# First weights in halves, ones ahead of them, and another order of the early pairs in four SwiGLUs

## The chip, the cores and the metric

The kernel runs on one core of one Trainium2 chip. The metric is the device time of one execution in microseconds. The engines are TensorE (PE in the profile, with PEld for its weight loads), VectorE (DVE), ScalarE (ACT), GpSimd (POOL) and SyncE (SP, which issues nearly all DMAs).

## The reference

A trunk of two layers over 768 tokens (512 of one group, 256 of another) with 1024 features. Each layer is a half SwiGLU, a mixer, and a half SwiGLU; a final RMSNorm ends it. The mixer of layer 0 is a gMLP gate beside windowed attention, that of layer 1 is a 2-D neighbourhood attention. Four SwiGLUs in all, with FF = 2816 hidden columns:

```python
def rmsnorm(x, g):
    x32 = x.astype(jnp.float32)
    y = x32 * lax.rsqrt(jnp.mean(x32 * x32, axis=-1, keepdims=True) + EPS)
    return y.astype(x.dtype) * g

def swiglu(h, wg, wu, wd):
    return (jax.nn.silu(h @ wg) * (h @ wu)) @ wd
...
# each half SwiGLU: x + 0.5 * swiglu(rmsnorm(x, g), wg, wu, wd)
```

## The kernel before

x is kept transposed as eight tiles x0 to x7 of 128 features by 768 tokens, worked on in two halves of H = 384 columns (HALVES). Every product is made of three fp32r matmuls: each operand is split into a high part and the rest, and high by high, low by high and high by low are summed in PSUM (mm3, L140). A weight tile of 128x512 is split by wsplit: ACT casts it to whi (L114), DVE subtracts to get wlo (L115).

In a SwiGLU (ffn) the hidden columns come as 11 pairs of two 128-column blocks, gate and up. A pair is a 2x2 block product (two feature halves, two token halves, two column blocks) done with seven products in place of eight. Its x operands are called b11, b21, t2, t3, n4, t1 and b22, each four tiles with a high part (b110h, ...) and a low part (b110l, ...); feed(m, 0) and feed(m, 1) make them for the two token halves. The weights of t2, t3, t1 and b22 are sums s1 to s4 of raw tiles (L609). One product is 24 matmuls of 128x384: two names, four feature tiles, three terms.

The operands carry the gains of the norm but not 1/rms, which is multiplied in later. norm_rt makes it: squares on ACT (L216, L219), added up on DVE (L220) into acc; a product with ones ("tok", norm_tok) sums over features; rsqrt is a chain of 128x3 operations on DVE (L265 to L276); norm_spread turns the result into diagonals (DVE L256 for the high part, ACT L254 for the rest) and spreads it over 128 partitions by a product onesr by diag in PE (the "spread"), which ACT copies to acc (L414). hidden(i, half) then multiplies the two finished PSUM banks by it on DVE: sg (L508) from the gate's, v (L510) from the up's, then silu on ACT and sg = sg * v (L511). These reads set the banks free.

Since 1/rms is late, the first EARLY = 4 pairs begin with b11 (p1, whose result ACT also copies to an SBUF tile, L524, and notes in copied) and b21 (p2), which accumulate in the banks "X", and only then hidden. Those are the stages that a generator yields between, and ORDER says whose stage comes next. There are four banks mm and four banks aux in PSUM; a pair takes two for X. Pair 3 takes aux for X, the others mm. After ORDER is through, the remaining products of pair 0, 1, ... follow, beginning with t2 and t3 in two further banks.

The order on PE is the order in which the code issues: self.t adds up a modelled time of the matmuls issued, and generators given to spawn (the norm's steps with their delays, second()) continue when their time has come. The order on DVE, ACT and SP is set by a scheduler with priorities (high_priority) and explicit followers (issue_after). second() makes the operands and squares of the second token half in the first SwiGLU. SP loads weights into four raw tiles (512 KB each); w tiles are five of each kind.

Of the kernel before, what the change touches and what calls it, by code (L numbers as in the profile page):

```python
# [9 lines left out]
F32 = mybir.dt.float32  # L10
# [3 lines left out]
AF = mybir.ActivationFunctionType  # L14
ALU = mybir.AluOpType

P = 128
D = 1024
KD = D // P
# [4 lines left out]
H = T // 2  # L24
# [6 lines left out]
KIND = {"l0f1": ("f", 0), "l0m": ("m0", 1), "l0f2": ("f", 2), "l1f1": ("f", 3), "l1m": ("m1", 4), "l1f2": ("f", 5)}  # L31
RPB_PAD = 24
NW = 5
DELAY0 = (7.0, 11.0)
DELAYM = (3.5, 7.5)
DELAY1 = (26.0, 12.0)
STEPS = (2.5, 1.5, 1.5)
RPB_W = 31 + 2 * RPB_PAD
NMASK = 8 * (24 + 32 + 24) + 4 * (40 + 40)
NE = 30  # L40
EARLY = 4
ORDER = (0, 1, 0, 1, 0, 2, 1, 3, 2, 3, 2, 3)

WTOTAL = 12 * D * FF + 8 * EARLY * P * D + D * 1792 + 2 * D * D + D * 3072 + D * 512
VTOK = (4.0,9.0)
# [6 lines left out]
class Trunk:  # L52
# [4 lines left out]
    def __init__(self, ctx, tc, aps, phases=PHASES):  # L57
        self.tc, self.nc, self.aps, self.phases = tc, tc.nc, aps, phases
        self.units = []
        self.woff = self.pi = 0  # L60
        self.t = 0.0
        self.chains = []
        self.spare = []
        self.first = []
        self.copied = []
        pool = lambda name, bufs, **kw: ctx.enter_context(tc.tile_pool(name=name, bufs=bufs, **kw))
# [22 lines left out]
        return side  # L89


    def raw(self, name, k0, nk, c0, n):
# [5 lines left out]
        raw = self.rawp.tile([P, nk * n], F32, tag="raw", name=f"raw{i}")  # L98
        self.nc.sync.dma_start(raw, src)
        if self.spare and i >= 16:  # L100
            self.spare.pop(0)()
        return raw.rearrange("p (k n) -> p k n", k=nk)

# [105 lines left out]
    def norm_add(self, m, c0, c1):  # L209

        nc = self.nc
        for a in range(c0, c1, H):
            b = min(a + H, c1)
            if a not in self.begun:
                self.begun.add(a)
                nc.scalar.activation(self.acc[:, a:b], self.x[m][:, a:b], AF.Square)  # L216
                continue
            sq = self.nt("sq")[:, : b - a]
            nc.scalar.activation(sq, self.x[m][:, a:b], AF.Square)  # L219
# [16 lines left out]

    def norm_spread(self, y, pool=None):

        nc = self.nc
        yh = self.sp.tile([P, 3], F32R, tag="yh", name="yh", bufs=2)  # L240
# [3 lines left out]
        rb = self.psum(self.aux, "aux")  # L244
        for i, t in enumerate((yh.bitcast(F32), yl)):
            diag = (
                pool.tile([P, H], F32R, tag="diag", name="diag", bufs=2)
                if pool and i
                else self.np_.tile([P, H], F32R, tag="nt", name="diag", bufs=3)
            )  # L250
            for b in range(3):
                c = slice(b * P, (b + 1) * P)
                if i:
                    nc.scalar.activation(diag[:, c], self.ident, AF.Copy, scale=t[:, b : b + 1])  # L254
                else:
                    nc.vector.tensor_scalar(  # L256
                        out=diag[:, c], in0=self.ident, scalar1=t[:, b : b + 1], scalar2=None, op0=ALU.mult
                    )
            self.mmul(rb[:, :H], self.onesr, diag, i == 0, i == 1)
        return rb[:, :H]  # L260

    def rsqrt(self, y, src, scale, v, h, it):

# [20 lines left out]
    def norm_half(self, h, d0=1.8, d1=4.0):  # L284

        c0, c1 = HALVES[h]
        yield d0
        with self.tc.high_priority():
            y = self.norm_tok(self.acc, c0, c1)
        yield d1  # L290
        with self.tc.high_priority():
            self.r[h] = self.norm_spread(y)

# [103 lines left out]
    def second(self):  # L397

        for n in (1, 2):
            while len(self.copied) < 2:  # L400
                yield 0.2
            with self.tc.issue_after(self.copied[1]):
                for m in [i // 2 + (0 if i % 2 else 4) for i in range(KD)]:
                    if n == 1:
                        self.feed(m, 1)
                    else:
                        self.norm_add(m, H, T)
        self.half_done(1)

    def norm_rt(self, h):  # L410

        yield from self.norm_half(h, *(DELAY1 if h else DELAY0))
        c0, c1 = HALVES[h]
        self.nc.scalar.copy(self.acc[:, c0:c1], self.r[h])  # L414
        self.scales.add(h)

    def ffn(self, pre):
        nc = self.nc
# [41 lines left out]
        def pair(p):  # L460

            early = p < EARLY
            names = ("gate", "up")
            a = {}

# [6 lines left out]
            h = hs[p] = {}  # L472
# [105 lines left out]
            last = (p1, p6, p2, p7, p4, p5, p3)  # L578
# [15 lines left out]
        kind = self.following[0]  # L594
# [814 lines left out]
    def build(self):  # L1409
        nc = self.nc  # L1410
        self.cp.tile([P, 96], F32, tag="space", name="space")
        self.ident = self.cp.tile([P, P], F32, tag="ident", name="ident")
        make_identity(nc, self.ident)
        self.ones = self.cp.tile([P, P], F32, tag="ones", name="ones")
        nc.gpsimd.memset(self.ones, 1.0)
# [3 lines left out]
        nc.scalar.dma_start(self.gains, self.aps["gains"])  # L1419
        self.ngains = self.cp.tile([P, 64], F32, tag="ngains", name="ngains")[:, : KD * len(NORMS)]  # L1420
        nc.gpsimd.tensor_scalar(out=self.ngains, in0=self.gains, scalar1=-1.0, scalar2=None, op0=ALU.mult)
        self.x = [self.xp.tile([P, T], F32, tag=f"x{m}", name=f"x{m}") for m in range(KD)]
        todo = [KIND[p] for p in self.phases] + [("last", 6)]
        kind = todo[0][0]
        if kind == "f":
            self.ffn_open("right")
            self.ffn_tiles()
# [1 line left out]
        elif kind != "last":  # L1429
            self.mixer_tiles("right")  # L1430
        self.norm_begin(todo[0])
        for h, (c0, c1) in enumerate(HALVES):
            for m in range(KD):
                nc.sync.dma_start(self.x[m][:, c0:c1], self.aps["x"][m, :, c0:c1])
                if not (h and kind == "f"):
                    self.final(m, c0, c1)
                if h == 0 and m % 4 == 3 and kind == "f":
                    pre = f"{self.phases[0][:2]}_ffn{self.phases[0][3]}"
# [126 lines left out]
```

## Time and profile before

| | |
|---|---|
| median of 3 runs | 2632.54 us (2632.37 to 2633.5) |
| profiled execution | 2634.87 us, span 2633.1 us, mean granted clock 0.99 |
| busy: PE, PEld, DVE, ACT, POOL | 97%, 95%, 86%, 52%, 3% |
| mean DMA rate | 84 GB/s over the span |
| first product of b11 in the first and in the fourth SwiGLU | 9.38 us, 2126.11 us |
| first spread in the second and in the third SwiGLU | 785.04 us, 1271.40 us |

A timeline row gives the start and the duration in us, the engine, the line, the operation with output <- inputs and shape, and in brackets the idle time before it with what ended it. A row of the waits gives the total, the count and the longest. A row of the windows gives, for a stretch, the busy us of PE, PEld, DVE, ACT and POOL with counts, then the granted clock of PE, the share of the DMA engines and GB/s.

### The profile page before, as it was taken

The numbers are of one execution on the slowest core, as the hardware profiler recorded it, in microseconds if no ns is written. First come the engines' busy times: TensorE is split into PE (matmuls) and PEld (weight loads), VectorE is DVE, ScalarE is ACT, GpSimd is POOL, SyncE is SP. The second block draws the span as 40 slices with busy tenths as digits, with TensorE's granted clock in tenths as the row PEclk, the third lists the DMA queues.
The fourth block names the chain that finished last, engine by engine and source line by source line (L and its number), as shares of the span: only waits on it lengthen the run. The fifth ranks groups of instructions, "written<-read, shape, count | busy, mean of one in ns | idle before, by whom it ended". The sixth has DMA issues, their size and how long they took to land.

```text
span 2633.1 us, 41175 instructions
## 1 busy us (share of the span) xinstructions
PE 2561.3 (97%) x15094; PEld 2491.3 (95%) x15094; DVE 2267.8 (86%) x4793; ACT 1365.6 (52%) x2851; POOL 88.0 (3%) x172
## 2 busy tenths in 40 slices
PE   7999999998999999999999999999999999999997
PEld 7999999987899999999999999989998989999997
DVE  8998889889779988898999888886777699988886
ACT  7544444555655544454654544454545465454443
POOL 0000000000100000000000000001222100000000
PEclk9999999999999999999999999999999999999998
DMA  5423222421223222222322222232221332222221
GB/s 168 133 78 103 71 81 65 145 87 37 89 77 97 81 81 77 68 75 86 96 81 81 73 73 74 88 111 63 63 63 40 105 104 81 81 71 74 68 87 54
DMA packets 83898, 218.99 MB, mean 83 GB/s; under 512 B 20080, under 2 KB 32880, under 8 KB 83696
## 3 DMA queue, kind: packets, MB, share of 16 engines
q1 hardware_dynamic: 83552, 216.34, 26.5%
q8 instruction: 118, 1.93, 0.3%
q14 instruction: 84, 0.69, 0.1%
q10 hardware_dynamic: 144, 0.03, 0.0%
HBM read 206.90 MB, written 15.07 MB: 84 GB/s over the span
## 4 chain that ended last, share of the span: by engine, by line
PE 86%; DVE 9%; ACT 2%; DMA 2%; issue 1%; SPq 0%; DVEq 0%; ACTq 0%
PE ps_mm L140 54%; PE ps_aux L140 31%; DMA raw<-in_w 1%; DVE wlo L115 1%; PE ps_aux L144 1%; DVE s L609 1%; DVE xl L739 1%; ACT p L911 1%; DVE p L920 0%; DVE p L905 0%; DVE tl L197 0%; ACT whi L114 0%; ACT xh L738 0%; DVE ol L197 0%; DVE x L706 0%
## 5 line engine op out<-in xcount | busy, mean ns | idle before, releaser
L114 ACT CAST whi<-s 128x512 fp32r<-128x512 f32 x496 | 304.9, 621 | 390.6 <-DVE s L609 133.1
L114 ACT CAST whi<-raw 128x512 fp32r<-128x512 f32 x512 | 311.0, 619 | 257.8 <-PE ps_mm L140 116.8
L115 DVE TENSOR_TENSOR wlo<-s,whi 128x512 fp32r<-128x512 f32 x496 | 337.0, 685 | 61.1 <-ACT whi L114 60.8
L115 DVE TENSOR_TENSOR wlo<-raw,whi 128x512 fp32r<-128x512 f32 x494 | 337.5, 691 | 28.3 <-ACT whi L114 24.1
L140 PE MATMUL ps_aux<-dt,whi 128*128 128x384 f32 x864 | 219.3, 334 | 2.1 <-ACT whi L114 2.1
L140 PE MATMUL ps_mm<-db,whi 128*128 128x384 f32 x864 | 219.2, 334 | 0.0
L140 PEld LDWEIGHTS ps_aux<-dt,whi 128*128 128x128 f32 x864 | 156.0, 188 | 2.4 <-ACT whi L114 2.4
L140 PEld LDWEIGHTS ps_mm<-db,whi 128*128 128x128 f32 x864 | 156.1, 188 | 0.0
L140 PE MATMUL ps_mm<-xh,whi 128*128 128x512 f32 (+1 forms) x416 | 147.4, 354 | 3.8 <-ACT xh L738 3.8
L140 PE MATMUL ps_aux<-dt,wlo 128*128 128x384 f32 x432 | 144.4, 334 | 0.3 <-DVE wlo L115 0.3
L140 PE MATMUL ps_mm<-db,wlo 128*128 128x384 f32 x432 | 144.4, 334 | 0.0
L140 PE MATMUL ps_mm<-xl,whi 128*128 128x512 f32 (+1 forms) x416 | 142.3, 342 | 1.1 <-DVE xl L739 1.1
L140 PE MATMUL ps_mm<-xh,wlo 128*128 128x512 f32 (+1 forms) x416 | 142.1, 341 | 0.0
L609 DVE TENSOR_TENSOR s<-raw 128x512 f32<-128x512 f32 x124 | 85.0, 686 | 23.0 <-DMA raw<-in_w 22.9
L499 DVE TENSOR_TENSOR u<-ps_aux,u 128x384 f32<-128x384 f32 x176 | 97.0, 551 | 2.8 <-PE ps_aux L140 2.6
L609 DVE TENSOR_TENSOR s<-raw,raw 128x512 f32<-128x512 f32 x124 | 83.7, 686 | 18.2 <-DMA raw<-in_w 18.0
L140 PE MATMUL ps_aux<-dh,whi 128*128 128x384 f32 x384 | 97.6, 335 | 0.6 <-DVE x L706 0.6
L911 ACT ACTIVATE p<-p,st 128x256 f32<-128x256 f32 (+3 forms) x144 | 68.9, 480 | 55.0 <-DVE st L909 54.9
L494 ACT COPY u<-ps_mm 128x384 f32<-128x384 f32 x176 | 83.5, 474 | 24.2 <-PE ps_mm L140 24.0
L661 DVE TENSOR_TENSOR x<-ps_aux,x 128x384 f32<-128x384 f32 x160 | 86.0, 552 | 9.3 <-PE ps_aux L140 9.2
L140 PEld LDWEIGHTS ps_mm<-xh,whi 128*128 128x128 f32 x416 | 79.9, 192 | 14.1 <-ACT xh L738 4.9
L140 PE MATMUL ps_mm<-oh,whi 128*128 128x384 f32 x256 | 88.1, 344 | 4.6 <-DVE x L888 4.0
(486 smaller groups left out, 8058.2 us busy)
## 6 DMA issues: line engine op xcount, KB each, us to landing
raw<-in_w SPq DMA_DIRECT2D x350, 512.0 KB, 3.7
xdm<-x SPq DMA_DIRECT2D x16, 384.0 KB, 2.3
x<-in_x SPq DMA_DIRECT2D x16, 192.0 KB, 5.5
x<-xdm SPq DMA_DIRECT2D x8, 384.0 KB, 3.4
xold<-xdm SPq DMA_DIRECT2D x8, 384.0 KB, 3.0
out_y<-y SPq DMA_DIRECT2D x8, 384.0 KB, 2.4
tab<-skew SPq DMA_DIRECT2D x8, 256.0 KB, 4.8
raw<-in_w SPq DMA_DIRECT2D x8, 256.0 KB, 2.6
```

What stands on the lines that cost most here:

```text
L114: nc.scalar.copy(hi, src)
L115: (eng or nc.gpsimd).tensor_tensor(out=lo, in0=src, in1=hi.bitcast(F32), op=ALU.subtract)
L140: self.nc.tensor.matmul(out, lhsT=lhsT, rhs=rhs, start=start, stop=stop, **kw)
L144: self.nc.tensor.transpose(out, src, self.ident)
L494: nc.scalar.copy(e[n, out], bank[key, n])
L499: nc.vector.tensor_tensor(out=t, in0=bank[key, n], in1=t, op=ALU.add)
L609: f = lambda o, x, y, op: self.nc.vector.tensor_tensor(out=o, in0=x, in1=y, op=op)
L661: nc.vector.tensor_tensor(out=o, in0=ps, in1=o, op=ALU.add)
L739: nc.vector.scalar_tensor_tensor(out=lo, in0=src, scalar=gain, in1=hi.bitcast(F32), op0=ALU.mult, op1=ALU.subtract)
L911: nc.scalar.activation(outs[i], outs[i], AF.Exp, bias=nm[:, i : i + 1], accum_out=sm[:, i : i + 1])
```

## The change

- The weights of pairs 0 and 1 in the first SwiGLU come as eight halves of 256 KB into the same four raw tiles: the first on ACT's DMA queue ahead of all else, the other three first halves on SP between x3 and x4, the second halves behind x7. Fourteen matmuls of ones by ones (128x128) run in an aux bank ahead of the first product; the cast that makes onesr moves from DVE to ACT.
- norm_spread is cut in two: diags (DVE and ACT) is issued with the tok step, spread (PE) later. The delays differ for the first SwiGLU (DELAYS, DELAYT) and the later ones (DELAY0).
- second() is queued behind the fourth copy of a p1 and behind the first 1/rms (rooted). In the first SwiGLU the b11 weights' splits are queued behind squares (HOLD), and b21's have no priority.
- ORDER changes: pair 2 does b11 and b21 in a row in aux banks, pair 3 does both in mm banks after hidden of pairs 0 and 1.

```diff
-DELAY0 = (7.0, 11.0)
+DELAY0 = (7.0, 13.0)
+DELAYS = (11.6, 8.5)
+WARM = 14
+HOLD = (0, 3, 4, 5)
...
+DELAYT = (22.0, 12.0)
...
-ORDER = (0, 1, 0, 1, 0, 2, 1, 3, 2, 3, 2, 3)
+ORDER = (0, 1, 0, 1, 2, 2, 0, 1, 3, 2, 3, 3)
...
     def norm_spread(self, y, pool=None):
...
+        return self.spread(self.diags(y, pool))
+
+    def spread(self, diags):
+
+        rb = self.psum(self.aux, "aux")
+        for i, diag in enumerate(diags):
+            self.mmul(rb[:, :H], self.onesr, diag, i == 0, i == 1)
+        return rb[:, :H]
...
         yield d0
         with self.tc.high_priority():
-            y = self.norm_tok(self.acc, c0, c1)
+            diags = self.diags(self.norm_tok(self.acc, c0, c1))
         yield d1
         with self.tc.high_priority():
-            self.r[h] = self.norm_spread(y)
+            self.r[h] = self.spread(diags)
...
-            while len(self.copied) < 2:
+            while len(self.copied) < 4 or not self.rooted:
                 yield 0.2
-            with self.tc.issue_after(self.copied[1]):
+            with self.tc.issue_after(self.copied[3]), self.tc.issue_after(self.rooted[0]):
...
-        yield from self.norm_half(h, *(DELAY1 if h else DELAY0))
+        yield from self.norm_half(h, *((DELAY1 if len(self.rooted) > 1 else DELAYT) if h else DELAY0 if self.rooted else DELAYS))
...
-                    mm = key == "Y" or key == "X" and p != EARLY - 1
+                    mm = key == "Y" or key == "X" and p != EARLY - 2
...
-                with self.tc.high_priority() if early and (b in ("b11", "b21") or b == "t2" and p == EARLY - 1) else nullcontext():
+                with ExitStack() as stack:
+                    if fresh and b == "b11":
+                        stack.enter_context(self.tc.issue_after(self.squares[HOLD[len(self.copied)]]))
+                    if early and (b == "b11" or b == "b21" and not fresh or b == "t2" and p == EARLY - 1):
+                        stack.enter_context(self.tc.high_priority())
                     st = self.wsplit(w, nc.vector)
...
-        nc.vector.tensor_copy(self.onesr, self.ones)
...
+            def first(i, k, eng=None):
+                name = pre + ("gate", "up")[i % 2]
+                self.raw(name, 4 * k, 4, i // 2 * 2 * P, P, raws[i][:, k * 512 : k * 512 + 512], eng)
+
+            first(0, 0, nc.scalar)
+        nc.gpsimd.memset(self.ones, 1.0)
+        nc.scalar.copy(self.onesr, self.ones)
...
+            ps = self.psum(self.aux, "aux")
+            for _ in range(WARM):
+                nc.tensor.matmul(ps[:, :P], lhsT=self.onesr, rhs=self.onesr, start=True, stop=True)
...
-                    self.first += [self.raw(f"{pre}_w_{n}", 0, KD, m // 4 * 2 * P, P) for n in ("gate", "up")]
+                    for i in range(4):
+                        if m > 4 or i:
+                            first(i, m // 4)
```

What this does to the order on the engines is shown at three places.

PE in the first SwiGLU, before, from the spread to the first t2 matmul. The banks 495 and 702 are of mm, 549 of aux; 495 is pair 2's gate, 549 pair 3's, 702 pair 0's t2.

```order
L140 MATMUL ps_aux_473<-diag,onesr 128x384 x2
L140 MATMUL ps_mm_495<-b110h,whi_496 128x384
...
L140 MATMUL ps_aux_549<-b110h,whi_550 128x384
...
L140 MATMUL ps_mm_495<-b210h,whi_591 128x384
...
L140 MATMUL ps_aux_549<-b210h,whi_627 128x384
...
L140 MATMUL ps_mm_702<-t20h,whi_708 128x384
```

The same after; 482 is pair 2's gate, 591 pair 3's, 692 pair 0's t2.

```order
L146 MATMUL ps_aux_482<-b110h,whi_483 128x384
...
L146 MATMUL ps_aux_482<-b210h,whi_528 128x384
...
L146 MATMUL ps_aux_542<-diag,onesr 128x384 x2
...
L146 MATMUL ps_mm_591<-b110h,whi_592 128x384
...
L146 MATMUL ps_mm_591<-b210h,whi_641 128x384
...
L146 MATMUL ps_mm_692<-t20h,whi_698 128x384
```

Before, the spread comes first, then b11 of pairs 2 and 3, then b21 of both. After, pair 2 is done whole in aux with the spread within it, and pair 3 whole in mm follows; its banks are those that pair 0's hidden sets free. The tok step moves 30 matmuls back, into b21 of pair 1.

DVE in the first SwiGLU, before, around the t2 weight of the gate (709). Bank 495 is pair 2's gate, 517 its up.

```order
L609 TENSOR_TENSOR s_706<-s_704,raw_694 128x512
L508 TENSOR_TENSOR sg<-ps_mm_495,acc 128x384
L115 TENSOR_TENSOR wlo_709<-s_706,whi_708 128x512
L609 TENSOR_TENSOR s_706<-raw_694,s_706 128x512
L510 TENSOR_TENSOR v<-ps_mm_517,acc 128x384
L609 TENSOR_TENSOR s_730<-raw_700 128x512
```

After, around the t2 weights of gate (699) and up (725); bank 591 is pair 3's gate, 613 its up.

```order
L531 TENSOR_TENSOR sg<-ps_mm_591,acc 128x384
L632 TENSOR_TENSOR s_694<-raw_686 128x512
L533 TENSOR_TENSOR v<-ps_mm_613,acc 128x384
L632 TENSOR_TENSOR s_696<-s_694,raw_684 128x512
L534 SCALAR_TENSOR_TENSOR sg<-sg,v 128x384
L373 SCALAR_TENSOR_TENSOR t11l<-tmp,gains,t11h 128x384
L121 TENSOR_TENSOR wlo_699<-s_696,whi_698 128x512
L632 TENSOR_TENSOR s_720<-raw_690 128x512
L373 SCALAR_TENSOR_TENSOR t12l<-tmp,gains,t12h 128x384
L632 TENSOR_TENSOR s_722<-s_720,raw_688 128x512
...
L121 TENSOR_TENSOR wlo_725<-s_722,whi_724 128x512
```

Before, the hidden rows around t2's first weight are pair 2's, one pair back; after, they are those of pair 3, the product just ahead of t2 on PE, and its v stands ahead of both t2 weights. Further up in the same list, ahead of pair 0's sg, 13 weight halves (wlo) stood before and 16 now.

DVE in the second SwiGLU, before, up to the t2 weight of the up (9040), where 8851 is pair 3's gate in aux and 8873 its up.

```order
L508 TENSOR_TENSOR sg<-ps_aux_8851,acc 128x384
...
L609 TENSOR_TENSOR s_9037<-s_9035,raw_9003 128x512
...
L197 TENSOR_TENSOR b220l<-tmp,b220h 128x384
...
L510 TENSOR_TENSOR v<-ps_aux_8873,acc 128x384
...
L115 TENSOR_TENSOR wlo_9040<-s_9037,whi_9039 128x512
```

After, up to the same weight (9073); 8930 is pair 3's up, now in mm.

```order
L533 TENSOR_TENSOR v<-ps_mm_8930,acc 128x384
...
L203 TENSOR_TENSOR b220l<-tmp,b220h 128x384
...
L534 SCALAR_TENSOR_TENSOR sg<-sg,v 128x384
...
L632 TENSOR_TENSOR s_9068<-raw_9038 128x512
...
L203 TENSOR_TENSOR b221l<-tmp,b221h 128x384
...
L632 TENSOR_TENSOR s_9070<-s_9068,raw_9036 128x512
...
L273 TENSOR_SCALAR diag<-ident,yh 128x128 x3
L632 TENSOR_TENSOR s_9092<-raw_9032,raw_9034 128x512
L121 TENSOR_TENSOR wlo_9073<-s_9070,whi_9072 128x512
```

Before, the weight follows right behind pair 3's v; after, b220l and b221l, three sums, sg and the diagonals of the second half's norm stand between. In the third SwiGLU the weight stands ahead of v after the change, in the fourth behind it with as much between.

More of the change, by code (lines that the diff above doesn't have):

```diff
@@ L65, in __init__ @@
         self.copied = []
+        self.rooted = []
         pool = lambda name, bufs, **kw: ctx.enter_context(tc.tile_pool(name=name, bufs=bufs, **kw))
@@ L89, in close, with raw @@
         return side
-    def raw(self, name, k0, nk, c0, n):
+    def raw(self, name, k0, nk, c0, n, raw=None, eng=None):
         i = len(self.units)
@@ L97, in raw @@
         self.woff += size
-        raw = self.rawp.tile([P, nk * n], F32, tag="raw", name=f"raw{i}")
-        self.nc.sync.dma_start(raw, src)
-        if self.spare and i >= 16:
+        if raw is None:
+            raw = self.rawp.tile([P, nk * n], F32, tag="raw", name=f"raw{i}")
+        (eng or self.nc.sync).dma_start(raw, src)
+        if self.spare and i >= 20:
             self.spare.pop(0)()
@@ L215, in norm_add @@
                 self.begun.add(a)
-                nc.scalar.activation(self.acc[:, a:b], self.x[m][:, a:b], AF.Square)
+                self.squares = [nc.scalar.activation(self.acc[:, a:b], self.x[m][:, a:b], AF.Square).ins]
                 continue
             sq = self.nt("sq")[:, : b - a]
-            nc.scalar.activation(sq, self.x[m][:, a:b], AF.Square)
+            self.squares.append(nc.scalar.activation(sq, self.x[m][:, a:b], AF.Square).ins)
             nc.vector.tensor_tensor(out=self.acc[:, a:b], in0=self.acc[:, a:b], in1=sq, op=ALU.add)
@@ L237, in norm_spread, with diags @@
     def norm_spread(self, y, pool=None):
+        return self.spread(self.diags(y, pool))
[4 more added lines that the diff above has]
+        return rb[:, :H]
+    def diags(self, y, pool=None):
         nc = self.nc
+        res = []
         yh = self.sp.tile([P, 3], F32R, tag="yh", name="yh", bufs=2)
@@ L243, in norm_spread @@
         nc.vector.tensor_tensor(out=yl, in0=y, in1=yh.bitcast(F32), op=ALU.subtract)
-        rb = self.psum(self.aux, "aux")
         for i, t in enumerate((yh.bitcast(F32), yl)):
@@ L255, in norm_spread @@
                 else:
-                    nc.vector.tensor_scalar(
+                    last = nc.vector.tensor_scalar(
                         out=diag[:, c], in0=self.ident, scalar1=t[:, b : b + 1], scalar2=None, op0=ALU.mult
                     )
-            self.mmul(rb[:, :H], self.onesr, diag, i == 0, i == 1)
-        return rb[:, :H]
+            res.append(diag)
+        self.rooted.append(last.ins)
+        return res
     def rsqrt(self, y, src, scale, v, h, it):
@@ L462, in pair @@
             early = p < EARLY
+            fresh = bool(self.first)
             names = ("gate", "up")
@@ L1411, in build @@
         self.cp.tile([P, 96], F32, tag="space", name="space")
+        todo = [KIND[p] for p in self.phases] + [("last", 6)]
+        kind = todo[0][0]
         self.ident = self.cp.tile([P, P], F32, tag="ident", name="ident")
-        make_identity(nc, self.ident)
         self.ones = self.cp.tile([P, P], F32, tag="ones", name="ones")
-        nc.gpsimd.memset(self.ones, 1.0)
         self.onesr = self.cp.tile([P, P], F32R, tag="onesr", name="onesr")
-        nc.vector.tensor_copy(self.onesr, self.ones)
         self.gains = self.cp.tile([P, 64], F32, tag="gains", name="gains")[:, : KD * len(NORMS)]
         nc.scalar.dma_start(self.gains, self.aps["gains"])
+        if kind == "f":
+            pre = f"{self.phases[0][:2]}_ffn{self.phases[0][3]}_w_"
+            raws = [self.rawp.tile([P, KD * P], F32, tag="raw", name=f"first{i}") for i in range(4)]
+            self.first += [t.rearrange("p (k n) -> p k n", k=KD) for t in raws]
+            def first(i, k, eng=None):
[4 more added lines that the diff above has]
+        nc.scalar.copy(self.onesr, self.ones)
+        make_identity(nc, self.ident)
         self.ngains = self.cp.tile([P, 64], F32, tag="ngains", name="ngains")[:, : KD * len(NORMS)]
@@ L1422, in build @@
         self.x = [self.xp.tile([P, T], F32, tag=f"x{m}", name=f"x{m}") for m in range(KD)]
-        todo = [KIND[p] for p in self.phases] + [("last", 6)]
-        kind = todo[0][0]
         if kind == "f":
@@ L1431, in build @@
         self.norm_begin(todo[0])
+        if kind == "f":
+            ps = self.psum(self.aux, "aux")
+            for _ in range(WARM):
+                nc.tensor.matmul(ps[:, :P], lhsT=self.onesr, rhs=self.onesr, start=True, stop=True)
         for h, (c0, c1) in enumerate(HALVES):
@@ L1437, in build @@
                 if h == 0 and m % 4 == 3 and kind == "f":
-                    pre = f"{self.phases[0][:2]}_ffn{self.phases[0][3]}"
-                    self.first += [self.raw(f"{pre}_w_{n}", 0, KD, m // 4 * 2 * P, P) for n in ("gate", "up")]
+                    for i in range(4):
+                        if m > 4 or i:
+                            first(i, m // 4)
             if h and kind == "f":
```

## The prediction

> **What bounds the kernel now.** I read the page first, then the waits and the windows where a SwiGLU begins, then single rows.
>
> ```profile
> PE 2561.3 (97%) x15094; PEld 2491.3 (95%) x15094; DVE 2267.8 (86%) x4793; ACT 1365.6 (52%) x2851; POOL 88.0 (3%) x172
> PE 86%; DVE 9%; ACT 2%; DMA 2%; issue 1%; SPq 0%; DVEq 0%; ACTq 0%
> PE ps_mm L140 <- ACT whi L114: 9.4, 1, 9.4
> PE ps_mm L140 <- ACT p L524: 5.5, 1, 5.5
> PE ps_mm L140 <- DVE sg L508: 3.4, 1, 3.4
> 0.00:20.00 20.00, 10.62 (x45) 10.40 (x46) 12.25 (x23) 14.25 (x28) 1.28 (x8) 1.00 0.75 264
> 20.00:40.00 20.00, 12.61 (x61) 11.96 (x59) 19.35 (x54) 17.88 (x40) 0.00 (x0) 0.83 0.39 121
> 40.00:60.00 20.00, 18.52 (x100) 18.52 (x101) 19.11 (x42) 11.20 (x23) 0.00 (x0) 0.91 0.48 131
> 775.00:800.00 25.00, 23.78 (x137) 23.41 (x137) 24.67 (x60) 22.85 (x48) 0.00 (x0) 1.00 0.42 118
> 2140.00:2160.00 20.00, 19.59 (x106) 19.62 (x107) 17.82 (x42) 10.99 (x22) 0.00 (x0) 0.91 0.37 106
> ```
>
> TensorE (PE) is busy 97% of 2633.1 us: some 72 us are left. The three waits (in us, of the first 60) are 18.3 of them, all at the first SwiGLU. The windows give busy us of PE, weight load, DVE, ACT, POOL, then the granted clock, the DMA share and GB/s: from 20 to 60 us DVE is busy 38.5 of 40 us, as it is 24.67 of 25 at the second SwiGLU. So at two starts PE waits for engines that hardly pause themselves, and a wait taken from PE pays only as far as DVE's own work comes sooner. The rows:
>
> ```profile
> 9.38 0.69 PE L140 MATMUL ps_mm<-b110h,whi 128*128 128x384 f32 x1 [9.38 <-ACT whi L114]
> 14.75 0.52 PE L140 MATMUL ps_mm<-b111l,whi 128*128 128x384 f32 x1
> 15.07 0.49 PE L140 MATMUL ps_mm<-b111h,wlo 128*128 128x384 f32 x1
> 31.12 0.69 PE L140 MATMUL ps_mm<-b210h,whi 128*128 128x384 f32 x1 [5.50 <-ACT p L524]
> 41.48 0.44 PE L140 MATMUL ps_mm<-b110h,whi 128*128 128x384 f32 x1 [3.38 <-DVE sg L508]
> 60.48 0.33 PE L140 MATMUL ps_mm<-t20h,whi 128*128 128x384 f32 x1
> 60.65 0.33 PE L140 MATMUL ps_mm<-t20l,whi 128*128 128x384 f32 x1
> 62.90 0.33 PE L140 MATMUL ps_mm<-t20h,wlo 128*128 128x384 f32 x1
> 3.42 1.28 ACT L354 ACT_TABLE_LOAD   x1 [3.42 <-DMA x<-in_x]
> 4.71 0.61 ACT L354 ACTIVATE b110h<-x,gains 128x384 fp32r<-128x384 f32 x1
> 8.71 0.62 ACT L114 CAST whi<-raw 128x512 fp32r<-128x512 f32 x1 [1.54 <-DMA raw<-in_w]
> 5.36 0.62 DVE L355 SCALAR_TENSOR_TENSOR b110l<-x,gains,b110h 128x384 fp32r<-128x384 f32 x1 [4.02 <-ACT b110h L354]
> 21.39 0.16 DVE L265 TENSOR_SCALAR sm<-ps_aux 128x3 f32<-128x3 f32 x1 [0.59 <-PE ps_aux L140]
> 36.06 0.68 DVE L115 TENSOR_TENSOR wlo<-raw,whi 128x512 fp32r<-128x512 f32 x1
> 36.66 0.55 DVE L197 TENSOR_TENSOR t31l<-tmp,t31h 128x384 fp32r<-128x384 f32 x1
> 39.87 0.61 DVE L362 SCALAR_TENSOR_TENSOR tmp<-x,gains,tmp 128x384 f32<-128x384 f32 x1
> 40.40 0.55 DVE L197 TENSOR_TENSOR n40l<-tmp,n40h 128x384 fp32r<-128x384 f32 x1
> 40.87 0.55 DVE L508 TENSOR_TENSOR sg<-ps_mm,acc 128x384 f32<-128x384 f32 x1
> 33.01 0.67 DVE L256 TENSOR_SCALAR diag<-ident,yh 128x128 fp32r<-128x128 f32 x3
> 2602.69 0.16 DVE L275 TENSOR_TENSOR sm<-sm 128x3 f32<-128x3 f32 x1
> 2602.89 0.16 DVE L276 SCALAR_TENSOR_TENSOR sm<-sm 128x3 f32<-128x3 f32 x1
> ```
>
> Prices from starts of neighbours: a warm matmul 0.173 us, a cold one 0.32; on DVE a weight half (wlo, or a sum s) 0.60, a fused 128x384 operation 0.53, a plain one 0.47, three diag pieces 0.6 (duration, less overlap), a small 128x3 operation 0.20 in a chain of its own (2602.69 to 2602.89).
>
> **First SwiGLU, the start.** Before, PE waits 9.38 us for whi, whose half megabyte is there at 8.71; x0 is there by 3.42, and 1.28 of table load follows. After, the table is loaded before x arrives, so b110h can run up to 1.28 earlier; I take half, since the first quarter megabyte moves beside x0, and put DVE's first piece at 4.7 instead of 5.36. The first quarter megabyte lands between x0 and the 8.71; on its own issuer ahead of x0 I put it near 5, so with b110h, a square and the cast the first product starts near 6.0: 3.4 earlier. A later landing costs its lateness once. The 18 matmuls from 9.38 to 15.07 are cold and take 2.7 us too long; the 14 ones may remove all of that or nothing, and I keep both ends.
>
> The row says more than five microseconds of cold running, after 9.38 of idleness. [...]
>
> **First SwiGLU, the middle.** The sum of squares' product (the "tok" step, sm at 21.39 before) stands 30 matmuls later. By 6.0 + 78 x 0.173 + 0.95 (what 21.39 holds beyond 9.38, 48 x 0.173 and the 2.7) it reaches DVE at 20.5 warm, 23.2 cold. DVE's rows ahead of it are 9 wlo, 8 fused and 8 plain, 13.4 us, done at 18.1 from 4.7: DVE idles 2.4 to 5.1, say 3 to 6 with small waits. The row that frees pair 0's bank (sg) has 16 wlo, 17 fused, 28 plain, 15 small and 3 diag ahead: 9.6 + 9.0 + 13.2 + 2.6 + 0.6 = 35.0. Before there were 13 wlo, 18 fused, 27 plain and the small ones at 0.07 between others, 31.8. So sg comes at 42.7 to 45.7, not 40.87. PE has only pair 2 (48 matmuls in aux) to do until then and is through at about 33 to 35.5: the waits of 5.50 and 3.38 become one of about 10, in front of pair 3, and it is cold after it. After sg (0.5) come pair 3's 48 matmuls, 8.3, and 1.5 to 2.7 of cold: pair 3 ends at 53.0 to 57.2.
>
> Then a new wait. In DVE's order the product v of pair 3, which needs pair 3's last matmul, stands ahead of both t2 weights: v 0.47, s 0.60, sg 0.47, t11l 0.53, wlo 0.60, then s, t12l, s, s, t13l, wlo, 3.46: the up weight's wlo ends 6.1 after pair 3, where PE would use it after 14 matmuls, 2.4. That costs PE 3.7 us. Before, the up weight stood ahead of that v, and PE ran from 41.48 through 62.90 without a stop. So that same matmul runs at 59.1 to 63.3 against 62.90: a gain of 3.8 to a loss of 0.4. I take the middle, **-1.7 us**. The loads that now queue on SP between x tiles and the later second() add nothing of their own: the same bytes and rows are in the sums, moved behind p1's copies.
>
> **The later SwiGLUs.** Here only the spread, the bank and the order change.
>
> ```profile
> 785.04 0.68 PE L140 MATMUL ps_aux<-diag,onesr 128*128 128x384 f32 x2 [1.22 <-DVE diag L256]
> 811.42 0.69 DVE L115 TENSOR_TENSOR wlo<-s,whi 128x512 fp32r<-128x512 f32 x1
> 813.10 0.33 PE L140 MATMUL ps_mm<-t20h,wlo 128*128 128x384 f32 x1
> 815.85 0.44 PE L140 MATMUL ps_mm<-t30h,wlo 128*128 128x384 f32 x1 [0.50 <-DVE wlo L115]
> 1271.40 0.44 PE L140 MATMUL ps_aux<-diag,onesr 128*128 128x384 f32 x1 [1.14 <-ACT diag L254]
> 2140.41 0.41 PE L140 MATMUL ps_mm<-b110h,whi 128*128 128x384 f32 x1 [2.70 <-DVE sg L508]
> ```
>
> Second: the spread moves 12 matmuls (2.1 us) back, past its wait of 1.22. But between pair 3's v and the up weight's wlo now stand b220l, sg, s, b221l, s, three diag, s and six small rows: with v and wlo 5.3 us, so PE waits 2.9; the 0.50 at 815.85 goes, since the t3 weights follow at once. 1.22 + 0.50 - 2.9 = **+1.2** (0 if v is reached with DVE ahead, +2 if saturated DVE is late as well). Before, that wlo starts at 811.42, 1.7 ahead of its use. Third: the same 1.14 goes and the up weight's wlo stays ahead of v: **-1.0** (-1.1 to 0). Fourth: the 2.70 goes, since pair 3 now comes after pair 0's bank is long free, and with it the cold time, 9% of the 20 us from 2140, 1.8; but v and the up weight's wlo are 6.1 apart there too, which takes back 3.7: **-0.8** (-0.8, or +1 where some of the wait for sg stays).
>
> **The sum.** -1.7 + 1.2 - 1.0 - 0.8 = -2.3 us, with ends of -5.7 and +3.4. The profiled execution took 2634.87 for its span of 2633.1, 2.3 above the median 2632.54; the difference is carried to the median: **2630.2**. The bound of 0.2% is 5.3 us, about what a measurement of this kernel can tell from no change.
>
> **The rivals.**
> - Faster, 0.36: DVE and ACT keep up. If the clock is warm from the ones and halves land early, DVE has at most half a microsecond of idleness: sg at 40.2, pair 3 ends at 50.5, the up weight is used at 56.6, 6.3 sooner; with the later three as above 6.8 in all, 2625.7. If also the waits behind v are shorter than I make them (each row moves if its input is early), another 3.7, 2.9 and 3.7 come back: -17.1, 2615.4. For it speaks that 18.3 us of waits stand at one place; against it that DVE is busy 19.35 of 20 us there.
> - Slower, 0.15: the single wait before pair 3 grows. The matmul of 62.90 is reached 17.2 after sg with little of the cold (0.5 + 8.3 + 2.3 + 6.1), so from sg at 45.7 on each microsecond is lost, and DVE's rows wait in turn on ACT casts (ACT is busy 17.88 of 20 us). With sg at 49.5 the first SwiGLU loses 3.8, the second 2, the fourth 1, the third gains nothing: 2639.3.
> - No gain at the start, 0.06: the halves land no sooner than 8.71 since 264 GB/s are moved already, and the ones warm nothing. The start's 3.4 is gone, and the rest about nets out: 2632.5.
>
> **The numbers.** The forecast has 0.43, of which 0.04 lies beyond -5.3. Faster 0.36 + 0.04 = 0.40; slower 0.15; within 0.2% 0.39 + 0.06 = 0.45. The range goes from most of the first rival, 2619, to most of the second, 2638; the forecast's own is 2626.8 to 2636.
>
> **What would show it.** Right: the first product near 6; one wait of about 10 us for sg in front of pair 3's first matmul, at 43 to 46; waits of PE for wlo at t2 in the first, second and fourth SwiGLU, of 1 to 3.7 us; no wait for diag at the spreads. Wrong: sg before 41 or after 47; t2 without waits; the first 18 matmuls' clock tells which end of the tok step holds.

## The result and the profile after

The changed kernel takes 2632.7 us (median of 14 runs, 2631.54 to 2638.09) where the kernel before, run beside it, takes 2634.17 (14 runs, 2631.62 to 2638.37). The ratio is 1.0000 with a 95% interval of 0.9993 to 1.0007: no difference that can be measured (the medians lie 1.5 us apart, which is inside it).

The page of the changed kernel, PE's busy time and the chain:

```profile
PE 2567.1 (97%) x15108; PEld 2496.5 (95%) x15108; DVE 2267.7 (86%) x4792; ACT 1365.6 (52%) x2852; POOL 87.1 (3%) x172
PE 86%; DVE 9%; ACT 2%; issue 1%; DMA 1%; POOL 0%; ACTq 0%; DVEq 0%; POOLq 0%
```

PE is busy longer by 5.8 us for the same products: 3.25 are the ones (row below); the rest was not taken apart. PE's waits in the first 66 us by releaser (the sum in us, the number of waits, the longest):

```profile
PE ps_aux L146 <- ACT p L547: 5.8, 1, 5.8
PE ps_aux L1468 <- ACT onesr L1453: 3.3, 1, 3.3
PE ps_mm L146 <- ACT whi L120: 2.3, 2, 1.9
PE ps_mm L146 <- DVE sg L531: 1.9, 1, 1.9
PE ps_mm L146 <- DVE wlo L121: 0.8, 2, 0.5
```

The windows that answer to those of before:

```profile
0.00:20.00 20.00, 16.69 (x82) 16.57 (x83) 13.23 (x24) 16.46 (x33) 1.19 (x8) 1.00 0.84 295
20.00:40.00 20.00, 14.24 (x73) 13.92 (x72) 17.76 (x48) 15.36 (x34) 0.00 (x0) 0.85 0.54 167
40.00:60.00 20.00, 15.06 (x77) 13.47 (x77) 19.69 (x39) 12.31 (x25) 0.00 (x0) 0.98 0.24 53
```

The 9.38 us at the start have become 3.3 and the ones, the 5.5 and 3.4 have become 5.8 and 1.9, and behind them stand a new 2.3 (for whi) and 0.8 (for wlo), together 3.1, all four waits at t2 of pair 0. In the third window PE works 15.06 us where it worked 18.52: most of what was won by 40 us is given back by 60. The rows of PE in the timeline (start, duration, and in brackets the wait ahead of it):

```profile
3.31 3.25 PE L1468 MATMUL ps_aux<-onesr 128*128 128x128 f32 x14 [3.31 <-ACT onesr L1453]
6.36 0.63 PE L146 MATMUL ps_mm<-b110h,whi 128*128 128x384 f32 x1
10.29 0.34 PE L146 MATMUL ps_mm<-b110h,whi 128*128 128x384 f32 x1
35.73 0.69 PE L146 MATMUL ps_aux<-b210h,whi 128*128 128x384 f32 x1 [5.76 <-ACT p L547]
44.80 0.45 PE L146 MATMUL ps_mm<-b110h,whi 128*128 128x384 f32 x1 [1.87 <-DVE sg L531]
55.31 0.44 PE L146 MATMUL ps_mm<-t20h,whi 128*128 128x384 f32 x1 [1.90 <-ACT whi L120]
59.73 0.44 PE L146 MATMUL ps_mm<-t20h,wlo 128*128 128x384 f32 x1 [0.47 <-DVE wlo L121]
811.74 0.45 PE L146 MATMUL ps_mm<-t20h,whi 128*128 128x384 f32 x1 [2.23 <-ACT whi L120]
812.89 0.69 PE L146 MATMUL ps_mm<-t20h,wlo 128*128 128x384 f32 x1 [0.54 <-DVE wlo L121]
872.17 0.44 PE L146 MATMUL ps_mm<-t20h,whi 128*128 128x384 f32 x1 [1.50 <-ACT whi L120]
2159.44 0.44 PE L146 MATMUL ps_mm<-t20h,whi 128*128 128x384 f32 x1 [1.70 <-ACT whi L120]
```

The rows of DVE in the same timeline:

```profile
22.61 0.16 DVE L283 TENSOR_SCALAR sm<-ps_aux 128x3 f32<-128x3 f32 x1 [0.74 <-PE ps_aux L146]
44.20 0.55 DVE L531 TENSOR_TENSOR sg<-ps_mm,acc 128x384 f32<-128x384 f32 x1
53.45 0.56 DVE L533 TENSOR_TENSOR v<-ps_mm,acc 128x384 f32<-128x384 f32 x1 [0.30 <-PE ps_mm L146]
58.99 1.28 DVE L121 TENSOR_TENSOR wlo<-s,whi 128x512 fp32r<-128x512 f32 x2
807.46 0.56 DVE L533 TENSOR_TENSOR v<-ps_mm,acc 128x384 f32<-128x384 f32 x1 [0.40 <-PE ps_mm L146]
812.16 0.68 DVE L121 TENSOR_TENSOR wlo<-s,whi 128x512 fp32r<-128x512 f32 x1
```

DVE's v of pair 3 at 53.45 and the up weight's wlo, begun 5.5 us later at 58.99, are the ends of the chain. The waits at t2 in the second (811.74, with v at 807.46 and the up weight's wlo at 812.16) and fourth SwiGLU (2159.44) are of the same kind. PE has rows that both kernels share: in each SwiGLU the first t2 matmul of pair 4's gate and that of pair 10's gate. From one such row to the next the time differs from before as follows, in us. In brackets stand the cold matmuls of each stretch (starts 0.32 us apart, where a warm one takes 0.173):

| stretch | changed kernel |
|---|---|
| first SwiGLU, to 195.17 (all times of stretches are those of the trace of before) | -1.9 (24, before 39) |
| the rest of the first, to 460.26 | 0.0 (0, before 0) |
| from 460.26 to 946.01, the second | +2.9 (17, before 0) |
| from 1208.09 to 1437.81, the third | -2.3 (0, before 0) |
| from 1699.89 to 2294.85, the fourth | +1.6 (28, before 18) |

Of the 17 cold matmuls in the second, seven stand behind the waits at t2 and ten behind a wait of 1.50 us at 872.17, which the kernel before has too (at 871.75), with none cold behind it. "First" below is the stretch to 195.17. The rest of the first SwiGLU has one larger wait, for a weight of the product with dt; it is the same here as before, but in some of the runs below it is longer and cold, and in two it is gone. The first row is of the kernel before, the second of the first experiment:

```profile
252.05 0.62 PE L140 MATMUL ps_aux<-dt,whi 128*128 128x384 f32 x2 [2.12 <-ACT whi L114]
250.63 0.62 PE L146 MATMUL ps_aux<-dt,whi 128*128 128x384 f32 x2 [2.76 <-ACT whi L120]
```

Why it moves is not shown. It is given as "the rest of the first" where it is not 0.

### The profile page after: what moved, and what is told of

It is laid out like the page before. It is cut to its first block, busy times and chain, and to the rows that moved or that the text cites. A ratio compares the mean times of both kernels' runs of the same rounds, so it can differ in the third digit from the quotient of the medians.

```text
span 2633.4 us, 41199 instructions
## 1 busy us (share of the span) xinstructions
PE 2567.1 (97%) x15108; PEld 2496.5 (95%) x15108; DVE 2267.7 (86%) x4792; ACT 1365.6 (52%) x2852; POOL 87.1 (3%) x172
## 4 chain that ended last, share of the span: by engine, by line
PE 86%; DVE 9%; ACT 2%; issue 1%; DMA 1%; POOL 0%; ACTq 0%; DVEq 0%; POOLq 0%
PE ps_mm L146 54%; PE ps_aux L146 31%; DVE wlo L121 1%; DVE s L632 1%; DVE x L684 1%; PE ps_aux L150 1%; DMA raw<-in_w 1%; DVE xl L762 1%; ACT p L934 1%; DVE p L943 0%; DVE p L928 0%; DVE tl L203 0%; ACT whi L120 0%; ACT xh L761 0%; ACT sq L225 0%
## 5 line engine op out<-in xcount | busy, mean ns | idle before, releaser
L121 DVE TENSOR_TENSOR wlo<-raw,whi 128x512 fp32r<-128x512 f32 x486 | 331.8, 690 | 24.2 <-ACT whi L120 20.3
L684 DVE TENSOR_TENSOR x<-ps_mm,x 128x384 f32<-128x384 f32 x160 | 86.3, 549 | 5.3 <-PE ps_mm L146 5.0
```

The source lines that it names most:

```text
L121: (eng or nc.gpsimd).tensor_tensor(out=lo, in0=src, in1=hi.bitcast(F32), op=ALU.subtract)
L684: nc.vector.tensor_tensor(out=o, in0=ps, in1=o, op=ALU.add)
```

## The experiments

All ratios are to runs of the kernel before beside them, and each stretch is from one profile. One cold stretch of ten matmuls is about 1.5 us (ten times the 0.147 between the two spacings), so a single stretch is no surer than that.

**The chain at t2 undone, the old order, the new order alone, no ones.** The first moves pair 3's hidden behind pair 0's t2:

```diff
-ORDER = (0, 1, 0, 1, 2, 2, 0, 1, 3, 2, 3, 3)
+ORDER = (0, 1, 0, 1, 2, 2, 0, 1, 3, 2, 3)
...
                 f()
+                if p == 0 and f is p6:
+                    next(stages[3])
```

> The changed kernel with one move: pair 3's hidden (its sg and v on DVE) is issued behind the t2 products of pair 0 instead of ahead of them, in all four SwiGLUs; nothing else. Theory A (the gain made at the starts is given back by the chain pair 3's last matmul, v, sums, wlo, t2): the waits of PE for whi and wlo at the first t2 products (3.1 us in the first SwiGLU, 2.8 in the second, 2.9 in the fourth) go, and the cold matmuls behind them; by the landmarks of the changed trace the loss between pair 3's end and pair 1's t2 is 4.7, 6.1 and 5.4 us in the three, so the time falls by 8 to 16 us, to 2617 to 2625. Theory B (DVE's work as a whole sets the starts, whatever stands first): as much waiting appears at t3, n4 or at pair 1's t2, and the time stays within 2 us of 2632.7.

Measured: 2627.87 us, ratio 0.9976 (0.9968 to 0.9985), faster by about 6 us, and less than the 8 to 16 of theory A. The second stretch is -1.4, the third -3.2, the fourth -4.3; the first stays at -2.1, and the rest of the first is +2.4. In the first SwiGLU PE still waits at t2, less:

```profile
54.36 0.44 PE L146 MATMUL ps_mm<-t20h,whi 128*128 128x384 f32 x1 [1.11 <-ACT whi L120]
55.44 0.45 PE L146 MATMUL ps_mm<-t20h,wlo 128*128 128x384 f32 x1 [0.46 <-DVE wlo L121]
115.03 0.52 PE L146 MATMUL ps_mm<-t20h,whi 128*128 128x384 f32 x1 [1.90 <-ACT whi L120]
```

So theory A holds in the second and the fourth, where no wait at pair 0's t2 above 0.5 us is left and 4.4 and 6.0 us are won against the changed kernel. In the first, theory B holds: what is saved at 54 us is lost again at pair 2's t2, at 115, in the wait and in seven cold matmuls behind it.

```diff
-ORDER = (0, 1, 0, 1, 2, 2, 0, 1, 3, 2, 3, 3)
+ORDER = (0, 1, 0, 1, 0, 2, 1, 3, 2, 3, 2, 3)
-                    mm = key == "Y" or key == "X" and p != EARLY - 2
+                    mm = key == "Y" or key == "X" and p != EARLY - 1
```

> The changed kernel with the order of the early pairs and the bank rule of before; halves, ones, the cut of the norm, delays and queueing stay as changed. Theory A: the chain at t2 is gone, as is what the order gains; the first SwiGLU keeps its 3 us earlier first product in part (-1 to -3), the second and third lose the diag waits only (-1.2, -1.1), the fourth is as before: 2627 to 2630. Theory B: the start's gain is swallowed by DVE in the first SwiGLU (0), the rest -2: 2630 to 2632.

Measured: 2634.51 us, ratio 1.0001 (0.9993 to 1.001). The first stretch is +2.0 and the second +3.5, worse than either theory (the third is -3.5, the fourth +0.4, the rest of the first -1.3). Three rows bear on it: the spread behind the tok step and the bank wait of the first SwiGLU, now one of 12 us, and a bank wait that is new in the second:

```profile
27.29 0.44 PE L146 MATMUL ps_aux<-diag,onesr 128*128 128x384 f32 x1 [1.56 <-DVE diag L273]
40.84 0.69 PE L146 MATMUL ps_mm<-b110h,whi 128*128 128x384 f32 x1 [12.16 <-DVE sg L531]
795.36 0.69 PE L146 MATMUL ps_mm<-b110h,whi 128*128 128x384 f32 x1 [2.26 <-DVE sg L531]
```

In the first SwiGLU the start's three microseconds go into the longer wait for sg: pair 3 starts at 40.84, 0.6 us earlier than before. Most of the +2.0 comes later, 2.3 us of it between pair 2's and pair 3's t2, where ten matmuls are cold behind a wait of 1.50; the same wait stands there before, with none cold. In the second the new wait for sg (2.26, against the 1.22 for diag that is gone) and 18 cold matmuls make up the +3.5.

```diff
 (in the kernel before)
-ORDER = (0, 1, 0, 1, 0, 2, 1, 3, 2, 3, 2, 3)
+ORDER = (0, 1, 0, 1, 2, 2, 0, 1, 3, 2, 3, 3)
-                    mm = key == "Y" or key == "X" and p != EARLY - 1
+                    mm = key == "Y" or key == "X" and p != EARLY - 2
```

> The kernel before with only the new order of the early pairs and the bank rule. Theory A: the later SwiGLUs behave as in the changed kernel (second +3, third -1 to -2, fourth +1.6 against before, with the spread's wait kept or not), the first has the t2 chain with its late start, +1 to +4: 2635 to 2639. Theory B: no difference beyond 2 us from 2633.

Measured: 2635.69 us, ratio 1.0004 (0.9995 to 1.0012), about +1 us by the ratio, as in theory B, though the median lies in theory A's range. First -1.5 with a first product at 9.57: the order alone brings nearly all that the changed kernel wins up to there, and the earlier start, the delays and the queueing together 0.3. (The rest of the first is +2.3.) Second -0.4, third +0.1, fourth -1.9. In the second SwiGLU there is no wait at pair 0's t2, and at its t3 the row of before is left:

```profile
816.68 0.44 PE L140 MATMUL ps_mm<-t30h,wlo 128*128 128x384 f32 x1 [0.50 <-DVE wlo L115]
```

Here DVE does the up weight's wlo right behind v. The expected +3 was wrong: the order alone makes no chain in the second SwiGLU; there the chain needs the later spread as well, which the next group bears out. In the first and the fourth PE does wait at t2 with the order alone, 1.7 and 1.6 us.

```diff
-WARM = 14
+WARM = 0
```

> The changed kernel without the fourteen matmuls of ones. In the changed trace 12 of the first products run cold, 18 before. [...]

Measured: 2634.3 us, ratio 1.0002 (0.9994 to 1.0011). The first product starts at 5.39 instead of 6.36, so the ones had stood in its way, and it runs cold until about 10.4 instead of 10.3. The first stretch is -2.2 against -1.9. The delay was not expected; the ones bring nothing that shows.

**Where the spread stands, and which queue binds.**

```diff
-DELAY0 = (7.0, 13.0)
+DELAY0 = (7.0, 11.0)
```

> The changed kernel with the later SwiGLUs' spread back where it stood: DELAY0 11.0 instead of 13.0, which puts it one to three matmuls into the first b21, 12 earlier; the first SwiGLU is untouched. In DVE's order of the second SwiGLU this also takes two of the sums and the diagonals out from between pair 3's v and the up weight of t2. Theory A: the waits of PE at the second SwiGLU's t2 (2.23 and 0.54 us) shrink by 1 to 2 us, the diag wait of about 1.2 comes back, and the cold stretch behind goes or stays with the idle; second SwiGLU +0.5 to +2 against before instead of +2.9, total 2630 to 2632. Rival: the later spread is worth its 1.2 us, total 2633 to 2634.

Measured: 2628.89 us, ratio 0.998 (0.9972 to 0.9989). The second stretch is +0.9 instead of +2.9, its waits at t2 are gone and the diag wait is back in part (0.62 and 0.33 us at 784 us); the third is -3.1, the fourth -3.6. The first, which this edit leaves as it is, is 0.0 against -1.9 in this profile, with ten cold matmuls behind the wait for sg: so much comes and goes. Theory A holds, and its total was set too high: with 1/rms earlier by the time of 12 matmuls no wait at pair 0's t2 is left in the second SwiGLU, and 1.6 instead of 2.9 us in the fourth.

```diff
-            while len(self.copied) < 4 or not self.rooted:
+            while len(self.copied) < 6 or not self.rooted:
...
-            with self.tc.issue_after(self.copied[3]), self.tc.issue_after(self.rooted[0]):
+            with self.tc.issue_after(self.copied[5]), self.tc.issue_after(self.rooted[0]):
```

> The changed kernel with second() queued behind the sixth p1 copy (pair 2's up) instead of the fourth, so that the second token half's operands and squares on ACT stand behind pair 2's p1 copies; only the first SwiGLU differs. Theory A: the wait of 5.76 us for ACT's p1 copy before pair 2's b21 goes, pair 2 is through near 36 instead of 42.7, but pair 3 still waits for sg (44.2 before) so a wait of 4 to 7 us appears there instead: DVE is the bound of this SwiGLU and its end moves by -1 to +1. Rival: the copy was the bound, the first SwiGLU ends 4 to 6 us sooner, total 2627 to 2629.

Measured: 2633.36 us, ratio 0.9997 (0.9988 to 1.0006). The wait of 5.76 for ACT's copy is gone, and this stands in its place:

```profile
43.21 0.69 PE L146 MATMUL ps_mm<-b110h,whi 128*128 128x384 f32 x1 [8.76 <-DVE sg L531]
76.92 0.87 PE L146 MATMUL ps_aux<-diag,onesr 128*128 128x384 f32 x2 [3.50 <-DVE diag L273]
```

sg comes 1.6 us earlier, PE waits for it longer, and the second half's 1/rms, now late, costs 3.5 more: the first stretch is +1.9. The rest of the first is -3.0, since the wait at dt is gone, so the whole SwiGLU is -1.1 against the changed kernel's -1.9. The copy was not the bound: theory A.

> The two moves together: pair 3's hidden behind pair 0's t2, and second() behind the sixth copy. Theory A (DVE bounds the first SwiGLU, the chain at t2 the later ones): as with the first move alone, 2625 to 2628. Rival: another 4 us less, 2621 to 2624.

The edit is that of the first and of this one. Measured: 2627.23 us, ratio 0.9972 (0.9962 to 0.9983), not to be told from the first move alone; the first stretch is +3.1 and the rest of the first -3.0 (the first move alone: -2.1 and +2.4), the fourth -5.8. Theory A.

> Pair 3's hidden behind pair 0's t2, and DELAY0 back at 11.0. Theory A: without the chain at t2 the earlier spread no longer helps, and its wait for diag (1.2 us each in the second and third SwiGLU) comes back: 1 to 2.5 us slower than with the first move alone, 2628 to 2630. Rival: 1/rms comes earlier, so sg does, and the time is 1 to 2 us less than with the first move alone.

Measured: 2628.14 us, ratio 0.9979 (0.997 to 0.9988); also not to be told from 0.9976. The second stretch is +1.0 against -1.4, with 10 cold matmuls against none, which is 1.5 us of the 2.4; theory A points the right way and its size is not shown. Each move alone brings 0.2%, and both together bring no more: they undo one and the same chain.

**What sets the first SwiGLU.**

```diff
-                    st = self.wsplit(w, nc.vector)
+                    st = self.wsplit(w, None if pre == "l0_ffn1" and p in (2, 3) and b in ("b11", "b21") else nc.vector)
```

> The first move's kernel (pair 3's hidden behind pair 0's t2), and in the first SwiGLU alone the eight weight subtractions of b11 and b21 of pairs 2 and 3 on POOL instead of DVE: 4.8 us off DVE, of which seven, 4.2 us, lie between the tok step and pair 0's sg. Theory A (DVE's work sets the first SwiGLU): sg comes 3 to 4 us earlier than 44.1, the wait in front of pair 3 goes, and the landmark at the first t2 of pair 4 (195.17 before, -2.1 with the first move alone) comes at -4 to -6; total 2622 to 2626. Rival: ACT's p1 copies or the products themselves set it, or POOL's subtractions are too slow for PE: the landmark stays at -2 or comes later.

Measured: 2637.0 us, ratio 1.0015 (1.0006 to 1.0024), the first stretch +7.5, the rest of the first +3.8, sg at 48.85. It tells nothing of the question, since beside POOL's subtractions (5.04 us for four) DVE itself was slower. DVE's small operations from 23 us on, with POOL busy from 21.96 to 27.0 (the same operations take 0.16 in the changed kernel):

```profile
23.42 1.11 DVE L284 TENSOR_SCALAR smi<-sm 128x3 int32<-128x3 int32 x1
24.56 1.21 DVE L287 TENSOR_SCALAR sm<-smi 128x3 int32<-128x3 int32 x1
25.69 0.15 DVE L290 TENSOR_SCALAR sm<-sm 128x3 f32<-128x3 f32 x1
25.81 1.21 DVE L292 TENSOR_TENSOR sm<-sm 128x3 f32<-128x3 f32 x1
27.05 0.16 DVE L293 TENSOR_TENSOR sm<-sm 128x3 f32<-128x3 f32 x1
```

The same question with less work instead of moved work:

```diff
-            nc.vector.tensor_tensor(out=self.acc[:, a:b], in0=self.acc[:, a:b], in1=sq, op=ALU.add)
+            if a == 0 or self.nxt[1]:
+                nc.vector.tensor_tensor(out=self.acc[:, a:b], in0=self.acc[:, a:b], in1=sq, op=ALU.add)
```

> The first move's kernel (pair 3's hidden behind pair 0's t2) with the seven additions of the second token half's squares left out on DVE in the first SwiGLU, so that half's 1/rms is that of one feature tile; all else runs. 3.3 us less on DVE, all ahead of pair 0's sg in its order. Theory A (DVE's work sets the first SwiGLU): sg comes 2.5 to 3.3 us earlier than 44.1 and the landmark at the first t2 of pair 4 comes 2 to 3.3 us earlier than the -2.1 of the first move alone: -4 to -5.5. Rival: ACT's copies or PE's own products set it; sg comes earlier, but the landmark stays within 1 us of -2.1.

Measured: 2626.71 us, ratio 0.9979 (0.997 to 0.9988). sg comes 3.3 us earlier, by all that was taken away, and the wait in front of pair 3 is gone:

```profile
40.76 0.55 DVE L532 TENSOR_TENSOR sg<-ps_mm,acc 128x384 f32<-128x384 f32 x1
```

The first stretch is -3.9 against -2.1: 1.9 us of the 3.3 reach it, just under theory A's bound, and PE's wait for ACT's copy (5.91) now stands alone. So DVE's work sets sg; of the stretch it sets a part, a little over half of what was taken away in this one pair of profiles (the rest of the first is +2.5 here and +2.4 there). In the whole time the 1.9 us can't be seen.

**How much of it the order needs.** Both edits of the order and the first move, on the kernel before:

> The kernel before with the new order and bank rule and with pair 3's hidden behind pair 0's t2, without halves, ones, the cut of the norm, the delays and the queueing of second(). Theory A: the order with this move is what pays, the start brings 0.3 us to the first SwiGLU and the spread's place 1 us each to the second and third: 2627 to 2630, second and third each 1 us slower than with the first move. Rival: the rest of the change is needed for it, 2631 to 2634.

Measured: 2632.03 us, ratio 0.9992 (0.9984 to 1.0001), in the range of the rival. First -1.9, the rest of the first +2.5, second +1.2, third +0.4, fourth -5.2. The first and the fourth do not need the rest of the change: with it they are -2.1 and -4.3. The second and third do: with it they are -1.4 and -3.2. The waits for diag (1.22 and 1.14 us) and for u (0.91 and 0.64 us), which stand in this run, are not there in the first move's.

**The same kernel again.**

> The changed kernel once more, for its profile alone. Theory A: the waits of PE repeat to 0.1 us, but the cold stretches behind waits of 1.5 to 2.3 us (at 813, 874, 2113, 2161 and 2221 us in the first profile) come and go from one execution to the next, so single landmarks differ by up to 1.6 us for each, and the times of one kernel spread over several microseconds. Rival: the clock follows the waits, and the same stretches are cold again.

Measured: 2632.73 us, ratio 1.0004 (0.9995 to 1.0013), and a profile with a span of 2637.0 against 2633.4. At t2 PE waits 2.23 and 0.54 us in the second SwiGLU and 1.72 and 0.47 in the fourth, as before. The window from 768 us, in the first profile of the changed kernel and then in the second (the granted clock stands third from the end):

```profile
768.00:776.00 8.00, 8.00 (x50) 8.00 (x49) 7.08 (x21) 5.10 (x10) 0.00 (x0) 1.00 0.07 16
```

```profile
768.00:776.00 8.00, 6.21 (x29) 6.12 (x28) 6.25 (x13) 3.77 (x8) 0.00 (x0) 0.79 0.00 0
```

A wait of 1.8 us for x stands in front of both (at 765.91 and 769.88). Behind one the clock stays full, behind the other ten matmuls are cold. The second stretch is +5.5 in this profile, and the span 3.6 us longer, for the same program. In the mixer too the clock differs: from 626 to 644 us it is 0.85 in the first profile and 0.67 in the second. Behind the 1.50 us at 872.17, cold in the first, none is cold in the second. Theory A; stretches of single profiles carry about 1.5 us for each cold stretch.

## Why the prediction was right

The forecast was 2630.2 with a range of 2619 to 2638 and the largest chance, 0.45, within 0.2%. The mechanism was found as forecast but for one wait that stood elsewhere; two terms were mis-sized, and that the total came so near is in part luck. Step by step:

- **The start.** The first product came at 6.36 (forecast 6.0), the tok step reached DVE at 22.61 (20.5 to 23.2), sg ran at 44.20 (42.7 to 45.7), and the up weight's t2 matmul at 59.73 (59.1 to 63.3). The first SwiGLU gained 1.9 us, 1.7 forecast. The no-gain rival at the start was wrong about the halves, which landed early, and, as far as the runs show, right about the ones.
- **One wait in front of pair 3.** Wrong in its place: 5.76 us of it stood one product earlier, before pair 2's b21, for ACT's p1 copy, which ran behind the second half's operands, and 1.87 before pair 3. The step that failed is that of "PE has only pair 2 to do until then", which did not look at ACT's queue for that copy. The moved second() showed that it makes little difference: without that wait PE waits 8.76 us for sg instead of 7.63 in two parts.
- **The wait behind v.** Right in mechanism: 3.1 us of waits at t2 in the first SwiGLU against 3.7 forecast, 2.8 in the second against 2.9, 2.9 in the fourth against 3.7. The experiment that takes it away wins about 6 us and confirms it for the second and fourth; in the first SwiGLU it is waited for elsewhere.
- **The later three.** Second +2.9 against +1.2: the term was mis-sized by the cold clock. 17 matmuls were cold there, 2.5 us at 0.15 each, and none before, ten of them behind a wait that the change doesn't touch; the waits alone net about 1.1. Third -2.3 against -1.0: the wait for diag goes, and so does one of 0.72 behind it which I had not counted. Fourth +1.6 against -0.8: I counted the 1.8 us of cold time as gone with the 2.70, but 28 matmuls were cold against 18 before, behind the new waits and behind a wait of 1.77 in the mixer that the change doesn't touch; ten are 1.5 us. Such cold time comes and goes: with second() behind the sixth copy the waits at t2 in the fourth are the same 2.9 us, none is cold behind them, and the stretch is -1.8.
- **The sum.** -2.3 forecast, no difference measured (0.9993 to 1.0007 is -1.8 to +1.8 us, so -2.3 lies just outside): the errors of the second and fourth term, 4.1 us together, were set off in part by the third's 1.3. Some slips of arithmetic weigh little: 15 small rows at 0.20 are 3.0 and not 2.6, 6.3 and the later three are 6.9 and not 6.8, and 1.22 + 0.50 - 2.9 has its sign turned round. None of the rivals happened. The faster one needed sg at 40.2 and it ran at 44.20, and its waits behind v were only 0.1 to 0.8 us shorter than the rows said; the slower one's sg did not pass 45.7. The 2632.5 of the no-gain rival is nearest to the measured 2632.7, though the start it was built on did gain: the loss came later.

**The ones and the cold stretches.** The fourteen ones took 3.25 us. With them PE was busy from 3.31 and the warm spacing came at 10.29, without them busy from 5.39 and at about 10.4: that the ones warm anything is not shown. Nor is what makes the first matmuls cold: the granted clock of the window from 0 to 20 us reads 1.00 in both kernels, with 12 matmuls cold in the changed kernel and 18 before. Later, matmuls ran cold behind waits of 1.50 us (at 872), 1.79 (at 770 in the repeated profile) and 2.23 with 0.54 behind it (at 812), and none did behind the 1.50 at 871.75 in the kernel before: waits of this length can cost a cold stretch, not always.

## What to carry to other kernels

Where a wait on a bank is removed, look at what stands in the consumer's own list between the freeing operation of the *last* product and the next weight: the new order moved pair 3's v in front of t2's weights, and about 6 us hung on a hidden stage that could wait. Best of what was run is the change with that stage moved behind t2, at 0.9976 (0.9968 to 0.9985), or 0.9972 (0.9962 to 0.9983) with second() later, which is the same. The one number DELAY0 back at 11.0 gives 0.998 (0.9972 to 0.9989) and is not to be told from either: the chain also goes where 1/rms comes earlier. An earlier start is worth little where another engine's work, here DVE's up to sg, has no slack: up to pair 4, 3 us of it became 0.3 beside the order alone, and 0.2 with the hidden stage moved in both.

## What the runs showed of the hardware

A short wait in PE can cost a cold stretch of ten matmuls (about 1.5 us) or none, for the same program and the same wait: none was cold behind 1.78 us for x in one profile, ten behind 1.79 in the other (768 us, above; the granted clock there was 1.00 and 0.79). The 14 runs of the changed kernel spread over 6.6 us, and their clocks differ the same way: the two slowest (2638.09 both) were granted 0.987 in the mean, the two fastest (2631.54 and 2631.84) 0.991; how much of the spread the cold stretches make was not shown. Beside POOL's four 128x512 subtractions (5.04 us) DVE was slower: of the four operations shown that ran while POOL was busy, three took 1.1 to 1.2 us in place of 0.16.
